# mLSTM heads 0 to 2: a head's squares are added on GpSimd before the f32 sums

## The chip, the cores and the metric

The kernel runs on one core of one Trainium2 chip. Its metric is the device time of one execution in microseconds; the kernel before takes 1200.73 us (median of three runs, 1200.3 to 1201.46). The core has TensorE (matmuls, called PE in the profile, with PEld for the loading of weights), VectorE (DVE), ScalarE (ACT), GpSimd (POOL) and SyncE (SP, which issues loads).

## The reference

The program is a two-layer encoder on 512 tokens of width 1024. Layer A mixes tokens by an mLSTM with four heads of width 192 beside a cross-attention on 256 memory tokens; layer B by band attention beside the same kind of cross-attention; each layer ends in a gated MLP with a causal convolution. The change touches the mLSTM alone. For each head and token it computes a numerator of 192 values and a denominator, divides, and normalises the 192 values by their root mean square:

```
num = einsum(s, v) + inter * einsum(q, c)          # 192 values a token
den = sum(s) + inter * einsum(q, n)
h   = num / maximum(abs(den), exp(-m))
hm  = h * rsqrt(mean(h * h) + EPS)                 # mean over the 192 values
out = hm * head_gain * sigmoid(o)
```

Division and normalisation together need two sums for each token: the sum of the squares of the 192 numerators, and the square of the denominator. The kernel computes one factor from both, as rsqrt(sum/192 + EPS * max(den^2, floor)), and multiplies the gated numerators with it.

## The kernel before

Activations lie with features in the partitions (128) and tokens in the columns (512). Matrices are f32, split into a high and a low part (`split`, L133: ScalarE casts the high part at L134, VectorE subtracts the low part at L135), and a product is three matmuls (`mm3`, L171, lines 173 to 175).

A head is the generator `mlstm_head(h)` (L1136). Its 192 values are one full tile of 128 rows and half a tile of 64, which it shares with its neighbour head. `weighted_scores` makes the weighted scores of a block of 128 key tokens (broadcast of the row terms at L1147, Exp at L1149, causal cut on GpSimd at L1151, score products, split). `products` (L1166) multiplies them with the values into two PSUM banks `nums`. Bank 0 holds 128 numerators. Bank 1 holds 64 numerators and, in its other 64 rows, 64 copies of the denominator, since the value tile has 64 columns of ones there. Which half is which depends on the head being odd; `rs` is the half with numerators.

Then come the steps that the change is about. ScalarE squares both banks (L1187), VectorE multiplies them with the output gate (L1189). TensorE sums the squares over the partitions, for four token tiles T: at L1194 and L1195 two f32 matmuls of 128x128 squares with a two-column constant `mcf` add up in `st`. Column 0 receives the sum of the 192 squares, column 1 the mean of the 64 squared copies of the denominator. `mcf[:, 0]` is 1 in column 0 for all rows; `mcf[:, 1]` and `mcf[:, 2]` have 1 in column 0 for the half with numerators and 1/64 in column 1 for the other. In the profile an f32 matmul is two instructions (two passes). From `st` VectorE computes the factor on 128x4 elements (L1199 to L1201, `rsqrt` at L217 with lines 220 to 226), and two diagonal matrices (L235). TensorE broadcasts them (`spread`, L244, matmuls at L248), and VectorE multiplies the gated numerators with the result (L1208) and splits it.

TensorE's gaps are filled with projections. `weave(job, filler, each)` (L204) advances the filler by `each` steps for every yield of the job, or by `each` times the number that is yielded. A step of a projection (`project`, L177) is three matmuls of 512 columns. The filler of heads 0 to 2 is one chain of 112 steps: query and key tiles with a convolution (`qk_tile`, L1095, taps at L1103, Silu at L1104), output gates (`o_tile`), and the queries of the memory attention (`head_queries`, L495, memsets on GpSimd at L498). Head 0 takes 1.4 steps a yield, head 1 1.125, the memory attention between heads 1 and 2 1.463, head 2 1.417; what is left runs behind head 2. Head 3 is filled with parts of the output projection. In this part of the program a scheduler orders the instructions of each engine by its estimates; the written order gives the priority. The MLPs later are ordered by hand.

Buffers are rings: 8 of the kind "t" (128x512 in SBUF: squares, Exp, convolution, diagonals), three PSUM banks "mm" for projections, three "sc", two "tr" (the `nums`).

Of the kernel before, what the change touches and what calls it, by code (L numbers as in the profile page):

```python
# [12 lines left out]
AF = mybir.ActivationFunctionType  # L13
ALU = mybir.AluOpType
AX = mybir.AxisListType

P = 128
D = 1024
S = 512
# [4 lines left out]
AH = 4  # L24
# [31 lines left out]
def trunk(  # L56
# [18 lines left out]
    nc = tc.nc  # L75
    V, A, G = nc.vector, nc.scalar, nc.gpsimd
# [10 lines left out]
    def sb(tag, shape, dtype=F32):  # L87
        count[0] += 1
        return pool.tile(shape, dtype, tag=tag, name=f"{tag}{count[0]}", bufs=bufs[tag])

    def ps(tag):
        count[0] += 1
        return psum.tile([P, S], F32, tag=tag, name=f"p{tag}{count[0]}", bufs=pbufs[tag])

    def small(n=4):
        return sb("s", [P, 32])[:, :n]
# [12 lines left out]
        out=maskf, in_=maskf, pattern=[[1, P]], base=0, channel_multiplier=-1,  # L109
# [10 lines left out]
    mcf = cpool.tile([P, 3, 2], F32, name="mcf")  # L120
# [8 lines left out]
    HEADS = (slice(0, HD), slice(HD, P))  # L129
# [3 lines left out]
    def split(hi, lo, src, on_act=True, pinned=False):  # L133
        high = A.copy(hi, src) if on_act else V.tensor_copy(hi, src)  # L134
        low = V.tensor_tensor(out=lo, in0=src, in1=f(hi), op=ALU.subtract)  # L135
        if pinned:
            pin(high)
            pin(low)
# [32 lines left out]
    def mm3(o, lh, ll, rh, rl, first, last, more=False):  # L171

        nc.tensor.matmul(o, lh, rh, start=first, stop=False, skip_group_check=more)  # L173
        nc.tensor.matmul(o, lh, rl, start=False, stop=False, skip_group_check=more)  # L174
        nc.tensor.matmul(o, ll, rh, start=False, stop=last, skip_group_check=more)  # L175
# [41 lines left out]
    def rsqrt(y, v):  # L217
        n = v.shape[-1]
        yi = y.bitcast(I32)
        V.tensor_scalar(yi, v.bitcast(I32), 1, None, op0=ALU.logical_shift_right)  # L220
        V.tensor_scalar(yi, yi, -1, 0x5F3759DF, op0=ALU.mult, op1=ALU.add)
        t = small(n)
        for _ in range(3):
            V.tensor_mul(t, y, y)
            V.scalar_tensor_tensor(t, t, -0.5, v, op0=ALU.mult, op1=ALU.mult)
            V.scalar_tensor_tensor(y, t, 1.5, y, op0=ALU.add, op1=ALU.mult)

    def diagonal(c):

        cs = [sb("s", [P, 32], F32R)[:, :TT] for _ in range(2)]  # L230
        split(*cs, c, on_act=False)
        dgs = []
        for c in cs:
            dg = sb("t", [P, S], F32R)
            V.tensor_tensor(  # L235
                out=dg.rearrange("p (a b) -> p a b", a=TT),
                in0=ident.unsqueeze(1).to_broadcast([P, TT, P]),
                in1=f(c).unsqueeze(2).to_broadcast([P, TT, P]),
                op=ALU.mult,
            )  # L240
            dgs.append(dg)
        return dgs

    def spread(dgs, tag):  # L244

        o = ps(tag)
        for i, dg in enumerate(dgs):
            nc.tensor.matmul(o, onesr, dg, start=i == 0, stop=i == 1)  # L248
        return o
# [262 lines left out]
    def head_scores(o, h, q, tsl, k, c, first, keys_first=False):  # L512

        for i, part in enumerate(q):
            a, b = part[h][:, tsl], k[h][:, c]
            if keys_first:
                a, b = b, a
            nc.tensor.matmul(o, a, b, start=first and i == 0, stop=i == 1)  # L518
# [491 lines left out]
    e, u, c, r = (cpool.tile([P, TT, AH], F32, name=f"gate{i}") for i in range(4))  # L1010
# [125 lines left out]
    def mlstm_head(h):  # L1136
        hp, odd = divmod(h, 2)
        sh = 3 * hp + 1
        full = 3 * hp + 2 * odd
        rs = slice(HD, P) if odd else slice(0, HD)  # L1140
        pt = sb("pt", [P, 5 * S], F32R)

        def weighted_scores(s):
            n = S - s * P
            sl = slice(s * P, (s + 1) * P)
            r = ps("sc")
            nc.tensor.matmul(r[:, :n], sels[s % 2][:, h, :], rp[s // 2][:, s * P :], start=True, stop=True)  # L1147
            e = sb("t", [P, S])
            A.activation(e[:, :n], r[:, :n], AF.Exp, bias=acol[:, s, h : h + 1])  # L1149

            G.affine_select(  # L1151
                out=e[:, :P], in_=e[:, :P], pattern=[[1, P]], base=0, channel_multiplier=-1,
                compare_op=ALU.is_ge, fill=0.0,
            )
            yield
            o = ps("sc")
            kf, qf = ks[full], qs[full]
            mm3(o[:, :n], kf[0][:, sl], kf[1][:, sl], qf[0][:, s * P :], qf[1][:, s * P :], True, False)
            head_scores(o[:, :n], odd, qs[sh], slice(s * P, S), ks[sh], sl, False, True)
            V.scalar_tensor_tensor(e[:, :n], o[:, :n], DH**-0.5, e[:, :n], op0=ALU.mult, op1=ALU.mult)  # L1160
            split(pt[:, RO[s] : RO[s + 1]], pt[:, 1280 + RO[s] : 1280 + RO[s + 1]], e[:, :n])
            yield

        nums = []

        def products(s):  # L1166
            if not nums:
                nums.extend(ps("tr") for _ in range(2))
            for o, c in zip(nums, (3 * P, 2 * P) if odd else (0, P)):
                mm3(  # L1170
                    o[:, s * P :], vh[hp][s][:, c : c + P], vl[hp][s][:, c : c + P],
                    pt[:, RO[s] : RO[s + 1]], pt[:, 1280 + RO[s] : 1280 + RO[s + 1]], s == 0, s == TT - 1,
                )
            yield

        yield from weighted_scores(0)
        yield from weighted_scores(1)
        yield from weighted_scores(2)
        yield from products(0)
        yield from weighted_scores(3)  # L1180
        yield from products(1)
        yield from products(2)
        yield from products(3)
        sqs = []
        for o, j, r in ((nums[0], full, slice(0, P)), (nums[1], sh, rs)):
            sq = sb("t", [P, S])
            A.activation(sq, o, AF.Square)  # L1187
            sqs.append(sq)
            V.tensor_tensor(out=og[j][r, :], in0=o[r, :], in1=og[j][r, :], op=ALU.mult)  # L1189
        yield  # L1190
        st = ps("sc")
        for T in range(TT):
            sl = slice(T * P, (T + 1) * P)
            nc.tensor.matmul(st[:, 2 * T : 2 * T + 2], sqs[0][:, sl], mcf[:, 0, :], start=True, stop=False)  # L1194
            nc.tensor.matmul(st[:, 2 * T : 2 * T + 2], sqs[1][:, sl], mcf[:, 1 + odd, :], start=False, stop=True)  # L1195
            yield 0.581
        st = st[:, : 2 * TT].rearrange("p (t c) -> p t c", c=2)
        z, fc = small(), small()
        V.tensor_tensor(out=z, in0=st[:, :, 1], in1=floor2[:, :, h], op=ALU.max)  # L1199
        V.tensor_scalar(z, z, EPS, 1e-35, op0=ALU.mult, op1=ALU.max)  # L1200
        V.scalar_tensor_tensor(z, st[:, :, 0], 1.0 / DH, z, op0=ALU.mult, op1=ALU.add)  # L1201
        rsqrt(fc, z)
        dg = diagonal(fc)
        yield 2.673
        fb = spread(dg, "sc")
        yield
        for j, r in ((full, slice(0, P)), (sh, rs)):
            V.tensor_tensor(out=og[j][r, :], in0=fb[r, :], in1=og[j][r, :], op=ALU.mult)  # L1208
            if mixes[j] is None:
                mixes[j] = sb("u", [P, S], F32R), sb("u", [P, S], F32R)  # L1210
            split(mixes[j][0][r, :], mixes[j][1][r, :], og[j][r, :])
# [8 lines left out]
    fill = chain(a_tiles(2), a_memory_queries(0), a_tiles(3, 4), a_tiles(5), a_memory_queries(1))  # L1220
    memkv = load_memory_kv(0)
    weave(mlstm_head(0), fill, 1.4)
    until(lambda: og[2] is not None, fill)
    weave(mlstm_head(1), fill, 1.125)
    until(lambda: memq[0] is not None, fill)
    weave(memory_attention(memq[0], memkv, 0, mixes), fill, 1.463, 4)
    until(lambda: og[4] is not None, fill)
    weave(mlstm_head(2), fill, 1.417)
    run(fill)
    reload_x()  # L1230
# [30 lines left out]
    for j in range(KT):  # L1261
        wh, wl = weights(rows(ffn_w_down[0], j * P, P, FT - LAST, FT), LAST, P)
        o = ps("mm")
# [252 lines left out]
```

## Time and profile before

| | us |
|---|---|
| median of three runs | 1200.73 |
| the profiled execution | 1202.01 |
| its span | 1200.3 |
| head 0, first row broadcast (L1147) to the second gated product (L1208) | 104.9 to 137.4 |
| sums of heads 0, 1, 2 and 3, first start | 125.0, 150.0, 206.3, 244.1 |

The profile shows one execution. A row of a timeline gives the start in us from the span's start, the duration in us, engine, line, operation, output<-input, shapes, and how many instructions are merged; in brackets the idle time ahead of it and what ended it. A row of waits gives who waited for whom, the total in us, how often, and the longest. A row of groups ends with the total busy time, the mean in ns, and the idle time ahead of the group.

### The profile page before, as it was taken

Reading aid. Unit: us, or ns where it says so; the run is one execution under the profiler, and the core shown is the slowest. Engines: PE = TensorE matmul, PEld = TensorE weight load, DVE = VectorE, ACT = ScalarE, POOL = GpSimd, SP = SyncE. Lnnn points to the kernel's source line nnn. Section 1 sums busy time; section 2 is a strip of 40 time slices with the busy share of each in tenths; the row PEclk is TensorE's granted clock in tenths of the full one; section 3 lists DMA queues with packets and bytes.
Section 4 is the critical chain, followed back from the end, with each engine's and each line's share of the span. In section 5 each row is a group of like instructions: output and inputs, shape, how many; then the busy total and the mean of one; then the engine's idle time right before and its main releaser. Section 6 shows DMA issues by size and latency. Waiting matters only on the chain.

```text
span 1200.3 us, 18274 instructions
## 1 busy us (share of the span) xinstructions
PE 1189.5 (99%) x6759; PEld 1041.8 (87%) x6759; DVE 971.2 (81%) x1810; ACT 708.8 (59%) x1276; POOL 123.5 (10%) x207
## 2 busy tenths in 40 slices
PE   9999999999999999999999999999999999999997
PEld 8988888888889989999888888888889989999986
DVE  6877687878978888888698888997897888888865
ACT  5546577654655555555565667775465555555545
POOL 1200101010021111111020000001001010111100
PEclk9999999999999999999999999999999999999999
DMA  8634222444275666665563323146326466666551
GB/s 287 210 88 123 54 54 57 146 140 132 70 175 161 155 157 161 151 144 128 146 195 111 91 70 100 54 130 202 115 88 149 106 140 141 141 138 137 121 158 70
DMA packets 199019, 155.97 MB, mean 130 GB/s; under 512 B 7864, under 2 KB 179346, under 8 KB 198930
## 3 DMA queue, kind: packets, MB, share of 16 engines
q1 hardware_dynamic: 183762, 119.73, 34.5%
q0 software_dynamic: 14592, 34.03, 13.8%
q8 instruction: 53, 0.87, 0.3%
q10 hardware_dynamic: 576, 1.05, 0.2%
q14 instruction: 36, 0.29, 0.1%
HBM read 126.27 MB, written 32.44 MB: 132 GB/s over the span
## 4 chain that ended last, share of the span: by engine, by line
PE 89%; DVE 6%; ACT 3%; DMA 2%; issue 1%; SPq 0%; ACTq 0%; DVEq 0%
PE pmm L173 14%; PE pmm L175 14%; PE pmm L174 14%; PE ptr L173 6%; PE ptr L175 6%; PE ptr L174 6%; PE pmm L783 6%; PE psc L175 4%; PE psc L173 4%; PE psc L174 4%; PE pmm L782 3%; PE psc L518 2%; DMA wr<-in_ffn_w_up_dram 1%; DVE u L135 1%; PE ptr L1343 1%; DVE wl L135 1%
## 5 line engine op out<-in xcount | busy, mean ns | idle before, releaser
L173 PE MATMUL pmm<-u,wh 128*128 128x512 f32 (+1 forms) x872 | 309.5, 355 | 0.1
L175 PE MATMUL pmm<-u,wl 128*128 128x512 f32 (+1 forms) x872 | 306.4, 352 | 0.0
L174 PE MATMUL pmm<-u,wh 128*128 128x512 f32 (+1 forms) x872 | 306.2, 351 | 0.1
L135 DVE TENSOR_TENSOR wl<-wr,wh 128x1024 fp32r<-128x1024 f32 (+3 forms) x172 | 199.4, 1161 | 55.8 <-ACT wh L134 53.9
L134 ACT CAST wh<-wr 128x1024 fp32r<-128x1024 f32 (+3 forms) x172 | 171.6, 1002 | 107.9 <-PE pmm L174 45.8
L175 PEld LDWEIGHTS pmm<-u,wl 128*128 128x128 f32 x872 | 164.5, 189 | 21.1
L174 PEld LDWEIGHTS pmm<-u,wh 128*128 128x128 f32 x872 | 164.7, 189 | 18.2 <-DVE u L135 0.8
L173 PEld LDWEIGHTS pmm<-u,wh 128*128 128x128 f32 x872 | 164.6, 189 | 18.0 <-ACT u L134 0.5
L173 PE MATMUL ptr<-u,wh 128*128 128x512 f32 x272 | 106.7, 392 | 0.0
L175 PE MATMUL ptr<-u,wl 128*128 128x512 f32 x272 | 106.1, 390 | 0.0
L174 PE MATMUL ptr<-u,wh 128*128 128x512 f32 x272 | 105.9, 389 | 0.0
L751 POOL DMA_DIRECT2D xspill<-t x64 | 55.5, 867 | 461.3 <-ACT t L750 450.3
L134 ACT CAST u<-pt 128x512 fp32r<-128x512 f32 x102 | 62.8, 616 | 45.9 <-DVE pt L873 45.8
L135 DVE TENSOR_TENSOR u<-pt,u 128x512 fp32r<-128x512 f32 x102 | 70.1, 688 | 11.2 <-ACT u L134 8.5
L175 PE MATMUL psc<-u,wl 128*128 128x256 f32 (+1 forms) x232 | 76.1, 328 | 0.2
L173 PE MATMUL psc<-u,wh 128*128 128x256 f32 (+1 forms) x232 | 76.2, 328 | 0.0
L174 PE MATMUL psc<-u,wh 128*128 128x256 f32 (+1 forms) x232 | 75.9, 327 | 0.0
L783 PE MATMUL pmm<-u,u 128*128 128x512 f32 x192 | 69.6, 397 | 0.0
L935 ACT ACTIVATE t<-t 128x512 f32<-128x512 f32 x34 | 21.5, 632 | 79.4 <-DVE t L658 79.4
L819 DVE TENSOR_TENSOR t<-t,pmm 128x256 f32<-128x256 f32 x72 | 30.1, 418 | 45.2 <-ACT t L817 45.1
L658 DVE SCALAR_TENSOR_TENSOR t<-t,cols,t 128x511 f32<-128x511 f32 x80 | 59.4, 743 | 3.7 <-ACT t L665 3.7
L750 ACT COPY t<-ptr 128x512 f32<-128x512 f32 x64 | 37.4, 585 | 42.1 <-PE ptr L175 42.1
(298 smaller groups left out, 2673.1 us busy)
## 6 DMA issues: line engine op xcount, KB each, us to landing
wr<-in_ffn_w_up_dram SPq DMA_DIRECT2D x54, 512.0 KB, 4.4
wr<-in_ffn_w_down_dram SPq DMA_DIRECT2D x38, 512.0 KB, 4.1
pt<-in_ffn_w_up_dram SPq DMA_DIRECT2D x34, 512.0 KB, 6.5
xspill<-t POOLq DMA_DIRECT2D x64, 256.0 KB, 5.3
wr<-in_a_w_in_dram SPq DMA_DIRECT2D x20, 512.0 KB, 3.9
xspill<-u POOLq DMA_DIRECT2D x32, 256.0 KB, 2.7
u<-xspill SPq DMA_DIRECT2D x32, 256.0 KB, 5.5
wr<-in_w_kv_dram SPq DMA_DIRECT2D x12, 512.0 KB, 3.9
```

The source lines that it names most:

```text
L134: high = A.copy(hi, src) if on_act else V.tensor_copy(hi, src)
L135: low = V.tensor_tensor(out=lo, in0=src, in1=f(hi), op=ALU.subtract)
L173: nc.tensor.matmul(o, lh, rh, start=first, stop=False, skip_group_check=more)
L174: nc.tensor.matmul(o, lh, rl, start=False, stop=False, skip_group_check=more)
L175: nc.tensor.matmul(o, ll, rh, start=False, stop=last, skip_group_check=more)
L518: nc.tensor.matmul(o, a, b, start=first and i == 0, stop=i == 1)
L658: V.scalar_tensor_tensor(acc[:, n:], src[:, : S - n], self.fw[:, c * FT + j : c * FT + j + 1], acc[:, n:], op0=ALU.mult, op1=ALU.add,)
L750: A.copy(t, o)
L751: G.dma_start(xspill[j], t, accum_op=ALU.add)
L782: nc.tensor.matmul(r[:, :H], w[1][:, k], p[i - 1][:, :H], start=False, stop=False, skip_group_check=True)
L783: nc.tensor.matmul(r, w[0][:, k], p[i - 1], start=False, stop=k == n - 1, skip_group_check=True)
L819: V.tensor_tensor(out=o, in0=o, in1=r[:, H:], op=ALU.add)
```

## The change

The two banks' squares are no longer summed by two matmuls a token tile. The squares of bank 1 stay in a 128-row tile `sq`. For heads 0 to 2, the squares of bank 0 are written in two halves of 64 rows into the rows of `sq` that hold numerators (tile `part`, rows `rs`), and GpSimd adds each half to them. Each of those 64 rows of `sq` then holds the sum of three squares, and one matmul a token tile is left. Head 3 keeps two tiles of squares and two matmuls.

Three things move with it. The gating products of VectorE stand behind all squares, bank 1 ahead of bank 0 in the built order. The yield ahead of the sums is 4 instead of 1 for heads 0 to 2. The sums of the four token tiles stand in one row, and the yield of 0.581 behind each of them is one of 2.324 behind the last.

```diff
-        sqs = []
+        sq = sb("t", [P, S])
+        A.activation(sq, nums[1], AF.Square)
+        terms = [(sq, mcf[:, 1 + odd, :])]
+        if h < AH - 1:
+
+            for half in HEADS:
+                part = sb("t", [P, S])
+                A.activation(part[rs, :], nums[0][half, :], AF.Square)
+                G.tensor_tensor(out=sq[rs, :], in0=sq[rs, :], in1=part[rs, :], op=ALU.add)
+        else:
+            part = sb("t", [P, S])
+            A.activation(part, nums[0], AF.Square)
+            terms.append((part, mcf[:, 0, :]))
         for o, j, r in ((nums[0], full, slice(0, P)), (nums[1], sh, rs)):
-            sq = sb("t", [P, S])
-            A.activation(sq, o, AF.Square)
-            sqs.append(sq)
             V.tensor_tensor(out=og[j][r, :], in0=o[r, :], in1=og[j][r, :], op=ALU.mult)
-        yield
+        yield 4 if h < AH - 1 else 1
         st = ps("sc")
         for T in range(TT):
             sl = slice(T * P, (T + 1) * P)
-            nc.tensor.matmul(st[:, 2 * T : 2 * T + 2], sqs[0][:, sl], mcf[:, 0, :], start=True, stop=False)
-            nc.tensor.matmul(st[:, 2 * T : 2 * T + 2], sqs[1][:, sl], mcf[:, 1 + odd, :], start=False, stop=True)
-            yield 0.581
+            for i, (t, c) in enumerate(terms):
+                nc.tensor.matmul(st[:, 2 * T : 2 * T + 2], t[:, sl], c, start=i == 0, stop=i == len(terms) - 1)
+        yield 2.324
```

## Prediction

> **What bounds the kernel now.** I read the page's busy shares and chain first, then the busy times of the stretch that holds the four heads, then what TensorE waited for in it.
>
> ```profile
> span 1200.3 us, 18274 instructions
> PE 1189.5 (99%) x6759; PEld 1041.8 (87%) x6759; DVE 971.2 (81%) x1810; ACT 708.8 (59%) x1276; POOL 123.5 (10%) x207
> PE 89%; DVE 6%; ACT 3%; DMA 2%; issue 1%; SPq 0%; ACTq 0%; DVEq 0%
> 84.00:256.00 172.00, 171.61 (x873) 144.27 (x872) 134.29 (x273) 110.69 (x191) 10.72 (x22) 1.00 0.31 87
> PE psc L173 <- ACT t L1149: 0.2, 1, 0.2
> PEld psc L173 <- ACT t L1149: 0.9, 2, 0.6
> PEld psc L248 <- DVE t L235: 0.6, 2, 0.3
> ```
>
> TensorE is busy 99% of the span and carries 89% of the chain. In the 172 us of the heads it is idle for 0.39 us at a granted clock of 1.00; its one wait is 0.2 us, the weight loads' longest are 0.6 and 0.3 us. So a matmul taken out here shortens the program by what it holds TensorE, and a wait put in lengthens it by as much: there is no idle time left to swallow one.
>
> **The matmuls that go.** This is TensorE around head 0's sums: the head's last numerator matmul, then projection matmuls (pmm), then the sums (L1194, L1195), two passes to an f32 matmul. Columns: start, duration.
>
> ```profile
> 122.76 0.28 PE L175 MATMUL ptr<-pt,u 128*128 128x128 f32 x1
> 122.88 0.44 PE L173 MATMUL pmm<-u,wh 128*128 128x512 f32 x1
> ...
> 124.78 0.40 PE L175 MATMUL pmm<-u,wl 128*128 128x512 f32 x1
> 125.01 0.28 PE L1194 MATMUL psc<-mcf,t 128*128 128x2 f32 x2
> ...
> 125.38 0.47 PE L173 MATMUL pmm<-u,wh 128*128 128x512 f32 x1
> 125.69 0.39 PE L174 MATMUL pmm<-u,wh 128*128 128x512 f32 x1
> ...
> 126.15 0.28 PE L1194 MATMUL psc<-mcf,t 128*128 128x2 f32 x2
> ...
> 126.96 0.47 PE L173 MATMUL pmm<-u,wh 128*128 128x512 f32 x1
> 127.28 0.39 PE L174 MATMUL pmm<-u,wh 128*128 128x512 f32 x1
> ...
> 127.74 0.28 PE L1194 MATMUL psc<-mcf,t 128*128 128x2 f32 x2
> 127.88 0.36 PE L1195 MATMUL psc<-mcf,t 128*128 128x2 f32 x2
> 128.10 0.47 PE L173 MATMUL pmm<-u,wh 128*128 128x512 f32 x1
> 128.42 0.39 PE L174 MATMUL pmm<-u,wh 128*128 128x512 f32 x1
> ```
>
> Between two projection matmuls lies 0.23 us (124.78 to 125.01). A group of four passes holds the next matmul up by 125.38 - 125.01 = 0.37, and the one behind it by 0.31 - 0.23 = 0.08: 0.45 us. The group of eight costs 126.96 - 126.15 = 0.81 and 0.32 - 0.23 = 0.09: 0.90. The third costs 0.36 + 0.09 = 0.45. Sum per head 1.80 us for 16 passes. Afterwards a head of 0 to 2 has eight passes in one row: 0.90. That takes off 3 x 0.90 = 2.70 us. Head 3 keeps 16 passes, but in one row instead of two, with one change-over (0.09) less. **Together -2.79 us**, all of it on the path.
>
> **The new way to the sums.** In the built order 21 projection matmuls now lie between a head's last numerator matmul and its sums, where 9, 6 and 9 lay before. Counted from the start of that last matmul (122.76), the sums' turn comes at 0.12 + (124.78 - 122.88) + 13 x 0.23 = 5.0 us, their weight load 0.23 before: 4.77. By then three ScalarE squares and two GpSimd adds must be done, in order. For prices on ScalarE, VectorE and GpSimd:
>
> ```profile
> 122.74 1.09 ACT L1187 ACTIVATE t<-ptr 128x512 f32<-128x512 f32 x2 [1.89 <-PE ptr L175]
> 155.00 1.28 ACT L1104 ACT_TABLE_LOAD   x1 [3.26 <-DVE s L1201]
> 156.29 0.63 ACT L1104 ACTIVATE t<-t 128x512 f32<-128x512 f32 x1
> 158.28 0.62 ACT L134 CAST u<-t 128x512 fp32r<-128x512 f32 x1
> L498 POOL MEMSET u<- 64x512 f32 x24 | 12.8, 533 | 46.9 <-PE pmm L175 23.5 <-PE psc L518 13.5 <-PE ptr L1365 7.9
> L108 POOL TENSOR_SCALAR_AFFINE_SELECT maskf<-maskf 128x128 f32<-128x128 f32 x1 | 0.3, 284 | 0.0
> L106 POOL MEMSET maskf<- 128x128 f32 x1 | 0.2, 204 | 0.0
> L1505 POOL MEMSET const-float32-1.0<- 128x1 f32 x1 | 0.1, 108 | 0.0
> 140.06 1.25 POOL L1151 TENSOR_SCALAR_AFFINE_SELECT t<-t 128x128 f32<-128x128 f32 x1 [0.57 <-ACT t L1149]
> 140.01 1.15 DVE L135 TENSOR_TENSOR pt<-t,pt 128x512 fp32r<-128x512 f32 x2
> ```
>
> No GpSimd add stands in the trace. From below, it is not cheaper than the memset of the same shape, which reads nothing: 0.53 us. From GpSimd's rows on 128 elements: the memset costs (204 - 108)/128 = 0.75 ns an element for writing, the select (284 - 108)/128 = 1.38 for reading one input and writing, so a read is 0.63. Two reads and a write give 2.01 ns x 512 + 108 = **1.14 us**, the value I take; two whole one-input passes, 2 x (1.38 x 512 + 108) = 1.63 us, are the upper end. [...]
>
> The other unknown is whether VectorE holds GpSimd up. The quoted select took 1.25 us instead of the 0.28 of L108; it ended at 141.31, just after two VectorE operations with both inputs in SBUF (140.01 to 141.16). So an add can lose what such an operation takes. [...]
>
> Heads 0 and 2. The square of the second bank can start at 0.28 + 0.02 = 0.30 and takes 0.60; with the spacing of L1187 (two in 1.09, so 0.49) the two halves end at 1.40 and 1.90. Adds: 1.45 to 2.59 and 2.64 to 3.78. One in each of these heads could last 1.63 us and still meet 4.77. VectorE's operations there read PSUM (the gating products, the convolution taps), the next split of weights comes behind them. **Cost 0**, covered by 0.95 us of matmuls; without that cover it would cost 2 x any excess over 1.63 us per head.
>
> Head 1. In the built order a table load and a Silu stand between the first and second square, and a cast between second and third. First square 0.30 to 0.90, table load 0.80 to 2.08, Silu 2.09 to 2.72, second square to 3.20, cast to 3.77, third square to 4.30 (each overlapping its forerunner by 0.1 as L1187 does). Adds: 3.25 to 4.39, and 4.44 to 5.58; the sums' weight load at 5.63 instead of 4.77: **0.9 us of wait**. VectorE's low half of that cast, both inputs in SBUF, is ready at 3.8, while the first add runs, and comes between the adds for another 0.6. I take 1.4 us, the ends being 0 (a table load that is through early) and 0.9 + 2 x 0.49 + 0.6 = 2.5.
>
> **Behind the sums.** The VectorE chain from the sums to the diagonals that the broadcast (L248) multiplies, head 1:
>
> ```profile
> 153.32 0.16 DVE L1199 TENSOR_TENSOR s<-psc,floor 128x4 f32<-128x4 f32 x1 [0.22 <-PE psc L1195]
> 153.40 0.74 DVE L1103 SCALAR_TENSOR_TENSOR t<-pmm,cols,t 128x510 f32<-128x510 f32 x1
> 154.06 0.16 DVE L1200 TENSOR_SCALAR s<-s 128x4 f32<-128x4 f32 x1
> 154.17 0.75 DVE L1103 SCALAR_TENSOR_TENSOR t<-pmm,cols,t 128x509 f32<-128x509 f32 x1
> 154.83 0.15 DVE L1201 SCALAR_TENSOR_TENSOR s<-psc,s 128x4 f32<-128x4 f32 x1
> 155.02 0.17 DVE L220 TENSOR_SCALAR s<-s 128x4 int32<-128x4 int32 x1
> 157.48 1.29 DVE L235 TENSOR_TENSOR t<-ident,s 128x512 fp32r<-128x512 f32 x2
> 158.69 1.22 DVE L135 TENSOR_TENSOR wl<-wr,wh 128x1024 fp32r<-128x1024 f32 x1
> 159.82 0.69 DVE L135 TENSOR_TENSOR u<-t,u 128x512 fp32r<-128x512 f32 x1
> ```
>
> Before, from L1199 to the end of the first diagonal: 157.48 + 0.68 - 153.32 = 4.84 us. Afterwards head 1 has inside this chain three taps (0.66 each with the step to the next), two splits of weights (1.13) and one of a cast (0.61): 0.08 + 2 x 1.13 + 3 x 0.66 + 2 x 0.11 + (157.48 - 155.02) + 0.61 + 0.68 = 8.29. TensorE has 36 projection matmuls to put there, 8.28 us. A wait of some **0.2 us** for L248. Head 0 keeps 29 of 30, head 2 its 24, with the same members in the chain; where the split of weights now stands earlier in head 2's, it waits for its high half: **0.2 us**. Ends for all three: 0 and 1.
>
> **What costs nothing.** Three more 64-row squares on ScalarE: 1.5 us, in a stretch where it works 110.69 of 172. The 12 filler steps that the longer yields bring forward: they are matmuls that come anyway, and head 2's order still has matmuls on both sides of its sums; were they used up, each missing step would bare 3 x 0.23 us of waiting. SP's loads keep their order. On GpSimd a head's adds stand ahead of the next head's selects and the memsets of queries; these are due only after L248, microseconds later. [...] The extra buffer of "t" adds no wait on the squares in the built order.
>
> **Sum.** -2.79 + 1.4 + 0.2 + 0.2 = -1.0 us. The profiled execution took 1202.01 us (span 1200.3); it would take 1201.0. The median of the three runs is 1200.73, 1.28 below that execution; I put the difference on it: **1199.7 us**.
>
> **Rivals.** First, no new wait: everything meets its turn in head 1 too, for instance because the table is loaded while TensorE still multiplies. Then -2.79 stays: 1197.9. Heads 0 and 2 with 0.95 us to spare speak for it; head 1's table load, which the order puts between its squares, against it.
>
> Second, slower: the add itself. If it takes g, head 1 waits 1.5 + 2 (g - 1.14), heads 0 and 2 each 2 (g - 1.63). With the 0.4 behind the sums the gain is used up at g = 1.6; at g = 2.0 the kernel is 0.2% slower; at 2.2 it is -2.79 + 0.4 + 3.6 + 2.3 = +3.5: 1204.2. For it: the select at 140.06 that took over four times its time; against it: the three GpSimd rows, which give 1.14.
>
> Third, the removed passes held nobody: then only the waits remain, +1.8, 1202.5. Against it: each group moves the next matmul by 0.36 to 0.81 us.
>
> **How the numbers follow.** About 0.2% (2.4 us) is what a measurement can tell from no change. The forecast, net -2.3 to +1, has 0.49; no wait 0.27; a slow add 0.16; removed passes free 0.05; 0.03 for waits elsewhere in the reordered stretch, above. Faster: the first rival, 0.27. Slower: the slow add and half of the rest, 0.18. Same: 0.55. The likeliest case's own range is 1198.4 to 1201.8. The range for 8 in 10 reaches from the full saving with no wait, 1197.8, to head 1's upper end (2.5) with 1 us at L248 and some of the slow add: 1202.6.
>
> **What would show it.** Sums: 20 f32 matmuls, not 32, in 40 passes; 8 passes of 0.81 us in heads 0 to 2. Six GpSimd adds of about 1.14 us. One wait of TensorE's weight load on GpSimd, near 150 us, of 0.9 to 1.5 us; none in heads 0 and 2. A small wait of L248 on L235 behind head 1. The stretch from 256 us on unchanged but earlier by 1 us. Wrong: adds over 1.63 us, waits on GpSimd in all three heads, or none at all.

## The result, and the profile after

The changed kernel takes 1202.38 us (median of 21 runs, 1201.33 to 1203.95); the kernel before, run beside it, 1200.74 (21 runs, 1200.16 to 1202.85). The ratio is 1.0012, with a 95% interval of 1.0007 to 1.0018: slower by 1.6 us. The forecast was 1199.7, so 1 us faster. The time lies inside the range and within the 0.2% that was called "same", but on the other side of zero, and above the 1198.4 to 1201.8 of the likeliest case. The profiled execution shown here took 1203.74 us, so it is one of the slower of the 21.

The page's opening lines of the changed kernel, its chain by engines, and the busy times of the stretch that was shown of before (time, then PE, PEld, DVE, ACT, POOL, then the granted clock, the DMA share and GB/s):

```profile
span 1202.0 us, 18245 instructions
PE 1190.2 (99%) x6735; PEld 1042.8 (87%) x6735; DVE 973.0 (81%) x1810; ACT 708.4 (59%) x1277; POOL 130.5 (11%) x213
PE 93%; DVE 3%; ACT 2%; issue 1%; DMA 0%; POOL 0%; SPq 0%; DVEq 0%; ACTq 0%
```

```profile
84.00:256.00 172.00, 169.77 (x837) 141.83 (x836) 132.85 (x269) 108.14 (x190) 17.74 (x28) 0.98 0.30 86
```

TensorE has 24 instructions fewer (6735 instead of 6759) and still bounds the kernel. But in the same 172 us it is now busy for 169.77 instead of 171.61, and the mean granted clock is 0.98, not 1.00. The waits of that stretch, TensorE's own first, then those of its weight loads (total, times, longest):

```profile
PE psc L1204 <- POOL t L1192: 1.6, 1, 1.6
PE ptr L174 <- DVE pt L135: 0.3, 1, 0.3
PE psc L248 <- DVE t L235: 0.2, 1, 0.2
PE pmm L174 <- DVE u L135: 0.2, 1, 0.2
...
PEld psc L1204 <- POOL t L1192: 2.0, 1, 2.0
PEld psc L248 <- DVE t L235: 0.9, 2, 0.6
```

One wait of the sums (L1204) on GpSimd, as forecast, in head 1 only. TensorE's timeline around it shows the rest of the story:

```profile
154.61 0.39 PE L175 MATMUL pmm<-u,wl 128*128 128x512 f32 x1
156.63 1.55 PE L1204 MATMUL psc<-mcf,t 128*128 128x2 f32 x8 [1.63 <-POOL t L1192]
158.04 0.78 PE L173 MATMUL pmm<-u,wh 128*128 128x512 f32 x1
158.62 0.63 PE L174 MATMUL pmm<-u,wh 128*128 128x512 f32 x1
...
163.31 0.63 PE L173 MATMUL pmm<-u,wh 128*128 128x512 f32 x1
163.74 0.45 PE L174 MATMUL pmm<-u,wh 128*128 128x512 f32 x1
164.02 0.39 PE L175 MATMUL pmm<-u,wl 128*128 128x512 f32 x1
```

The wait is 156.63 - 154.61 - 0.23 = 1.79 us. Behind it the projection matmuls start every 0.43 us instead of 0.23, until 163.7. The reason stands in the busy times by microsecond (granted clock third from the right):

```profile
155.00:156.00 1.00, 0.00 (x1) 0.00 (x0) 0.97 (x2) 0.97 (x2) 1.00 (x1) 1.00 0.00 0
156.00:157.00 1.00, 0.37 (x4) 0.37 (x4) 0.17 (x1) 0.60 (x1) 1.00 (x2) 1.00 0.00 0
157.00:158.00 1.00, 1.00 (x7) 1.00 (x7) 0.00 (x0) 0.00 (x0) 0.56 (x2) 0.50 0.00 0
...
163.00:164.00 1.00, 1.00 (x4) 0.78 (x3) 0.93 (x5) 0.13 (x1) 0.00 (x0) 0.58 0.03 8
164.00:165.00 1.00, 1.00 (x6) 0.82 (x5) 0.24 (x3) 0.00 (x0) 0.00 (x0) 1.00 0.00 0
...
1198.00:1199.00 1.00, 0.00 (x0) 0.00 (x0) 0.05 (x1) 0.02 (x1) 0.00 (x0) 0.53 0.07 29
```

The clock is halved from 157.00 to 163.84 (0.58 over the last microsecond is 0.84 of it at half). That is 6.84 us at half speed, 3.42 us lost: more than the wait itself. (The last row, after the last matmul, is used further down.)

The sums of the other heads, and head 3's:

```profile
127.09 0.95 PE L1204 MATMUL psc<-mcf,t 128*128 128x2 f32 x8
127.90 0.49 PE L173 MATMUL pmm<-u,wh 128*128 128x512 f32 x1
...
212.04 0.95 PE L1204 MATMUL psc<-mcf,t 128*128 128x2 f32 x8
212.85 0.49 PE L173 MATMUL pmm<-u,wh 128*128 128x512 f32 x1
...
246.65 1.84 PE L1204 MATMUL psc<-mcf,t 128*128 128x2 f32 x16
248.35 0.49 PE L173 MATMUL ptr<-u,wh 128*128 128x512 f32 x1
```

Eight passes take 0.81 us and wait for nothing in heads 0 and 2. Head 3's sixteen in one row take 1.70; before, two rows of 0.81.

GpSimd: the group of all six adds, and then the timelines of the engines that meet in head 1:

```profile
L1192 POOL TENSOR_TENSOR t<-t,t 64x512 f32<-64x512 f32 x6 | 8.0, 1340 | 24.6 <-ACT t L1191 15.4 <-issue 9.0
```

```profile
153.60 2.97 POOL L1192 TENSOR_TENSOR t<-t,t 64x512 f32<-64x512 f32 x2 [9.01 <-issue]
...
150.92 1.28 ACT L1104 ACT_TABLE_LOAD   x1
152.22 0.63 ACT L1104 ACTIVATE t<-t 128x512 f32<-128x512 f32 x1
152.87 0.59 ACT L1191 ACTIVATE t<-ptr 64x512 f32<-64x512 f32 x1
...
154.13 0.59 ACT L1191 ACTIVATE t<-ptr 64x512 f32<-64x512 f32 x1
...
154.14 1.30 DVE L135 TENSOR_TENSOR u<-t,u 128x512 fp32r<-128x512 f32 x1 [2.57 <-ACT u L134]
```

An add takes 1.28 to 1.29 us; in head 1 the second took 1.60 (six in 8.0 us). The table load and the Silu stand ahead of the second square, as the order said, and VectorE's low half of the cast ran beside the adds.

### The profile page after: what moved, and what is told of

Read it like the earlier page. It is cut to its first block, busy times and chain, and to the rows that moved or that the text cites. A ratio compares the mean times of both kernels' runs of the same rounds, so it can differ in the third digit from the quotient of the medians.

```text
span 1202.0 us, 18245 instructions
## 1 busy us (share of the span) xinstructions
PE 1190.2 (99%) x6735; PEld 1042.8 (87%) x6735; DVE 973.0 (81%) x1810; ACT 708.4 (59%) x1277; POOL 130.5 (11%) x213
## 3 DMA queue, kind: packets, MB, share of 16 engines
q10 hardware_dynamic: 576, 1.05, 0.2%
## 4 chain that ended last, share of the span: by engine, by line
PE 93%; DVE 3%; ACT 2%; issue 1%; DMA 0%; POOL 0%; SPq 0%; DVEq 0%; ACTq 0%
PE pmm L173 15%; PE pmm L174 15%; PE pmm L175 15%; PE ptr L174 6%; PE ptr L175 6%; PE ptr L173 6%; PE pmm L783 6%; PE psc L175 5%; PE psc L173 5%; PE psc L174 5%; PE pmm L782 3%; PE psc L518 2%; PE ptr L1352 1%; PE ptr L1373 1%; PE ptr L1374 1%
```

## The experiments

The stretch used below runs from head 0's first row broadcast (L1147) to the first broadcast L248 behind head 3's, which holds all four heads: 104.95 to 287.93 before, 182.98 us, and 104.30 to 290.54 after, 186.24. Its start lies between 103.66 and 105.92 us in the profiles of this document; the stretch itself doesn't contain that difference. All times are set against runs of the kernel before on the same chip.

First question: is it head 1's wait, and the clock behind it? Four edits of the changed kernel. In all of them the rest of the change stays: the gating products behind the squares, and each head's sums in one row.

**Head 1 as before, heads 0 and 2 changed.**

```diff
-        if h < AH - 1:
+        if h in (0, 2):
...
-        yield 4 if h < AH - 1 else 1
+        yield 4 if h in (0, 2) else 1
```

> The changed kernel, but head 1 keeps its two sums per token tile and its yield of 1; heads 0 and 2 keep the GpSimd adds. Theory A (head 1's wait of 1.8 us and the half clock behind it, 3.2 us, are the whole loss): no wait at the sums, granted clock 1.00 from 136 to 170 us, and two heads' saving of 0.90 each: about 1198.9 us. Rival B (the adds, or the reordering they bring, cost in every head): two thirds of the loss stay, about 1201.8 us.

1201.58 us against 1200.97, ratio 1.0000 (0.9992 to 1.0009). The wait is gone and the clock is 1.00 throughout. The stretch is 0.42 us shorter than before, where two heads' removed matmuls alone make 1.80. So the wait and the clock are not all of the loss: some 1.4 us went into the new order.

**Only head 1 changed.**

```diff
-        if h < AH - 1:
+        if h == 1:
...
-        yield 4 if h < AH - 1 else 1
+        yield 4 if h == 1 else 1
```

> Only head 1 has the GpSimd adds, heads 0 and 2 are as before. The order puts 18 matmuls instead of 21 between its numerators and its sums. Theory A: the wait is 2.5 us, the clock halves behind it for 3.2 us, less one saving of 0.90: 1200.7 + 2.5 + 3.2 - 0.9 = 1205.5 us. Rival B (a third of the loss in each head): 1201.3 us.

1201.36, ratio 1.0004 (0.9995 to 1.0013). The high figure was a miss for a reason of its own: in this order no table load stands between head 1's squares, so there is no long wait to test (0.4 us on the weight load). The stretch is 0.57 us longer than before, though a head's 0.90 was taken off: again about 1.5 us in the order.

**A longer yield ahead of head 1's sums:** 27 projection matmuls there instead of 21, and in a second kernel (a yield of 6) 24.

```diff
-        yield 4 if h < AH - 1 else 1
+        yield (4, 7, 4, 1)[h]
```

> The changed kernel with a yield of 7 instead of 4 ahead of head 1's sums: 27 projection matmuls instead of 21 lie before them (1.4 us more), and 31 instead of 36 behind them. Theory A: the wait at the sums shrinks from 1.8 to 0.4 us, the clock stays at 1.00, and of the 2.8 us saved about 1.9 remain, some 0.5 going to a later broadcast in head 1: 1198.9 us. Rival B (adds and reordering): no change against the changed kernel, 1202.4. Rival C (any wait at the sums halves the clock): about 1201.

> As with the yield of 7, but 6: 24 projection matmuls before head 1's sums, so a wait of about 1.1 us there. If the clock falls only behind waits near 1.8 us, 1199.5 us with a clock of 1.00; if 1.1 us is enough, about 3 us more, 1202.5, with a stretch at 0.50. Rival B: 1202.4 without such a stretch.

With 27, 1199.73 us (1199.32 to 1200.2), ratio 0.9991 (0.9982 to 1.0000). Little of the wait is left, and the clock is 1.00:

```profile
156.15 0.39 PE L175 MATMUL pmm<-u,wl 128*128 128x512 f32 x1
156.83 1.05 PE L1204 MATMUL psc<-mcf,t 128*128 128x2 f32 x8 [0.29 <-POOL t L1192]
```

Six matmuls, 1.4 us of work that comes anyway, turned 1.6 us above before into 1.2 below. With 24 the profile shows a wait of 157.04 - 155.69 - 0.23 = 1.12 us and a clock of 1.00:

```profile
155.69 0.39 PE L175 MATMUL pmm<-u,wl 128*128 128x512 f32 x1
157.04 1.05 PE L1204 MATMUL psc<-mcf,t 128*128 128x2 f32 x8 [0.96 <-POOL t L1192]
```

The median was 1200.62, but the runs spread from 1199.76 to 1203.69: six up to 1200.62, the others up to 3 us above. The mean granted clock is on record for every run; here it is 0.997 in the three slowest and 0.998 or 0.999 in the other eight. So a wait of 1 us costs more than its length in some executions only.

Second question: what is the order worth by itself, what the adds, and is the lower clock a chance of one profile? Four kernels.

**The changed kernel again.**

> The changed kernel once more, unchanged. Theory A (the wait at head 1's sums starts a drop of the granted clock, as in the profile after, and the two together cost 1.8 + 3.2 us): median 1202.4 again, and a profile with a wait of 1.6 to 1.9 us of L1204 on GpSimd near 155 us and, behind it, 3 to 7 us at a granted clock near 0.5. Theory B (that drop was a chance of one profiled execution, the loss lies elsewhere): the profile shows the wait and no drop, the median is 1202.4 all the same.

1202.50 (1201.5 to 1204.09), ratio 1.0013 (1.0004 to 1.0023). The profile has the same wait (156.97 - 154.96 - 0.23 = 1.78 us) and again the lower clock, for half as long, and later:

```profile
158.00:159.00 1.00, 1.00 (x6) 0.84 (x6) 0.94 (x2) 0.00 (x0) 0.00 (x0) 0.98 0.00 0
159.00:160.00 1.00, 1.00 (x4) 0.80 (x3) 1.00 (x3) 0.00 (x0) 0.00 (x0) 0.50 0.00 0
...
162.00:163.00 1.00, 1.00 (x5) 0.78 (x5) 0.83 (x6) 0.94 (x2) 0.00 (x0) 0.81 0.34 99
...
1196.00:1197.00 1.00, 0.00 (x0) 0.00 (x0) 0.75 (x1) 0.72 (x1) 0.00 (x0) 0.81 0.00 0
```

That is 158.96 to 162.38: 3.42 us at half, 1.71 lost. The stretch is 184.56 us, 1.58 longer than before; in the first profile it was 3.26, and the difference is one such piece.

**Two sums a tile as before, in the new order, without adds.**

```diff
-        if h < AH - 1:
+        if False:
```

> All heads keep two tiles of squares and two sums a token tile, and no GpSimd adds; what stays of the change is the order: longer yield ahead of the sums, the sums in one row. No matmul is removed, and TensorE has nothing to wait for. Theory A (the wait and the clock behind it are the loss): before's time less seven change-overs of 0.09, so 1200.3. Theory C (the new order by itself costs 1 to 2 us, which head 1 alone and head 1 left out both seemed to show): 1201.5 to 1202.5.

1202.92 (1202.25 to 1203.13), ratio 1.0017 (1.0008 to 1.0026). Nothing is removed, TensorE waits for no sum, the clock is 1.00, and it is 2.1 us slower. Theory C stands: the order costs. In the profile the cost is spread over many small delays, the longest of which are 0.50 us at head 3's product and this one in the memory attention (180.41 to 181.03, 0.39 too late):

```profile
180.41 0.39 PE L173 MATMUL pmm<-u,wh 128*128 128x512 f32 x1
181.03 0.70 PE L587 MATMUL ptr<-ident,t 128*128 128x128 f32 x4 [0.24 <-DVE t L578]
```

**The changed kernel without its adds.**

```diff
                 A.activation(part[rs, :], nums[0][half, :], AF.Square)
-                G.tensor_tensor(out=sq[rs, :], in0=sq[rs, :], in1=part[rs, :], op=ALU.add)
```

> The GpSimd adds are left out (the factor then lacks the squares of bank 0), all else stays: 16 passes less for heads 0 to 2 together with one row of sums, and the squares on ScalarE. Theory A: -2.79 and a wait of at most 0.4 us at head 1's sums, which come after the table load but no longer after two adds; no drop of the clock: 1198.2 to 1198.6. Theory C (the order costs 1 to 2 us): 1199.3 to 1200.3.

1199.22, ratio 0.9986 (0.9977 to 0.9995): 1.6 us faster, where 2.70 were taken off. Its stretch is 1.41 us shorter than before, so the order takes 1.29. TensorE's own waits there:

```profile
PE ptr L174 <- DVE pt L135: 0.3, 1, 0.3
PE psc L248 <- DVE t L235: 0.2, 1, 0.2
```

L248 starts 0.29 us late in head 1 and 0.36 in head 2, a product of head 3 0.49, all three waiting for VectorE; the rest is in pieces of 0.2 and less.

**One more add ahead of head 1's two.**

```diff
-                A.activation(part[rs, :], nums[0][half, :], AF.Square)
+                A.activation(part[rs, :], nums[0][half, :], AF.Square, scale=0.5**0.5 if h == 1 and half is HEADS[0] else 1.0)
+                if h == 1 and half is HEADS[0]:
+                    G.tensor_tensor(out=part[rs, :], in0=part[rs, :], in1=part[rs, :], op=ALU.add)
```

> One more GpSimd add of the same shape ahead of head 1's two (the half's square is scaled by 1/2 on ScalarE and doubled by an add, which leaves the sum as it is); TensorE's order is that of the changed kernel. The wait of L1204 should grow from 1.8 to 3.1 us. Theory A: the drop of the clock is there in the profile again, and as it lasts a fixed stretch the time is 1202.4 + 1.3 = 1203.7; should the drop grow with the wait, 1205. Theory B (nothing hangs on the wait but its own length): 1203.7 too, but no drop of the clock in the profile.

1204.26 (1202.36 to 1205.06), ratio 1.0027 (1.0017 to 1.0037). The profiled execution, 1202.41, is one of the two lowest, and it shows the wait without any drop of the clock:

```profile
154.63 0.39 PE L175 MATMUL pmm<-u,wl 128*128 128x512 f32 x1
157.74 1.05 PE L1206 MATMUL psc<-mcf,t 128*128 128x2 f32 x8 [2.71 <-POOL t L1194]
```

```profile
159.00:160.00 1.00, 1.00 (x6) 0.84 (x5) 1.00 (x1) 0.00 (x0) 0.00 (x0) 1.00 0.00 0
```

So a wait of 2.9 us need not lower the clock. The other six runs are 1.2 to 2.7 us longer than this one, and their granted clocks are lower: 0.995 to 0.997 in five of them and 0.998 in one, against 0.999 in the two lowest. One 1.71 piece is 0.0014 of the mean clock, so five of the six had one piece or two.

Third question: does a wait of that kind lower the clock where nothing else is changed? The kernel before, with GpSimd adds put ahead of head 1's sums. With one (and, in the other two kernels, a scale of 1/2 or 0.125**0.5 and a loop of two or three adds):

```diff
-            A.activation(sq, o, AF.Square)
+            A.activation(sq, o, AF.Square, scale=0.5**0.5 if h == 1 and j == sh else 1.0)
+            if h == 1 and j == sh:
+                G.tensor_tensor(out=sq, in0=sq, in1=sq, op=ALU.add)
```

> The kernel before with one GpSimd add put ahead of head 1's sums (the second square is scaled by 1/2 on ScalarE and doubled by the add, so the sum is as it was); TensorE's order is that of before, matmul for matmul, and no matmul is removed. By rows: the two squares end 1.4 to 1.9 us after the last numerator matmul, the add 1.3 later, the sums' turn comes at 1.5: a wait of 1.3 to 1.8 us. Theory A (a wait of this length also halves the granted clock for 0, 3.4 or 6.6 us, by where it falls): before + 1.5 + 0 to 3.2, median 1203.5 to 1204, runs spread over more than 2 us, and in most profiles some us near 0.5 behind the wait. Theory B (only the wait's own length): 1202.1 to 1202.7, clock 1.00.

> The kernel before with two GpSimd adds in a row ahead of head 1's sums (the second square is scaled by 1/4 and doubled twice), no matmul removed; TensorE's order differs by one step of a projection beside these sums. One add gave a wait of 0.57 us and +0.6; a second adds 1.29: a wait of 1.9 us. Theory A (a wait of this length lets the granted clock halve behind it in most executions, for 3.4 or 6.6 us): 1200.8 + 1.9 + 1.4 = 1204.1, the runs spread over more than 2 us, the lowest near 1202.5. Theory B (a wait costs its own length): 1202.7, runs within 1.5 us.

> As before, with three adds: a wait of 3.0 to 3.2 us. Theory A: 1200.8 + 3.1 + 1.8 = 1205.7, the lowest near 1203.8, spread over more than 2 us. Theory B: 1203.9, runs within 1.5 us.

One add: 1201.41 against 1200.80, ratio 1.0006 (0.9997 to 1.0014), clock 1.00; the wait was only 0.57 us (the sums on the first square alone still come before it), so it didn't yet test theory A. Two adds: 1204.29 against 1201.70, ratio 1.0019 (1.0010 to 1.0028). Three: 1206.78, ratio 1.0042 (1.0028 to 1.0056, from five runs). Two adds, TensorE's timeline and the busy times:

```profile
149.92 0.40 PE L174 MATMUL pmm<-u,wh 128*128 128x512 f32 x1
151.29 0.38 PE L1198 MATMUL psc<-mcf,t 128*128 128x2 f32 x2 [0.98 <-POOL t L1190]
```

```profile
153.00:154.00 1.00, 1.00 (x7) 0.91 (x5) 0.10 (x1) 0.00 (x0) 0.00 (x0) 0.72 0.31 52
...
156.00:157.00 1.00, 1.00 (x4) 0.80 (x3) 0.83 (x5) 1.00 (x1) 0.00 (x0) 0.57 0.00 0
```

and three:

```profile
151.95 0.40 PE L173 MATMUL pmm<-u,wh 128*128 128x512 f32 x1
154.84 0.38 PE L1198 MATMUL psc<-mcf,t 128*128 128x2 f32 x2 [2.49 <-POOL t L1190]
```

```profile
157.00:158.00 1.00, 1.00 (x5) 0.75 (x5) 0.93 (x4) 0.00 (x0) 0.00 (x0) 0.65 0.05 12
...
160.00:161.00 1.00, 1.00 (x4) 0.77 (x4) 0.83 (x6) 0.66 (x2) 0.00 (x0) 0.64 0.00 0
```

Waits of 1.14 and 2.66 us, shorter than expected, and behind each a piece at half clock: 153.44 to 156.86 and 157.30 to 160.72, 3.42 us both. The balance of the stretch, in us against the 182.98 of before (the wait beyond the 0.23 spacing; half of the time at half clock; the rest is what remains):

| kernel | stretch | removed | wait | clock | rest |
|---|---|---|---|---|---|
| before, one add | +0.62 | 0 | 0.57 | 0 | 0.05 |
| before, two adds | +2.92 | 0 | 1.14 | 1.71 | 0.07 |
| before, three adds | +4.49 | 0 | 2.66 | 1.71 | 0.12 |
| changed, first profile | +3.26 | -2.70 | 1.79 | 3.42 | 0.75 |
| changed, again | +1.58 | -2.70 | 1.78 | 1.71 | 0.79 |
| changed, a third add | +1.72 | -2.70 | 2.88 | 0 | 1.54 |
| changed, 24 matmuls ahead | -0.31 | -2.70 | 1.12 | 0 | 1.27 |
| changed, 27 matmuls ahead | -1.05 | -2.70 | 0.45 | 0 | 1.20 |
| changed, no adds | -1.41 | -2.70 | 0 | 0 | 1.29 |

In the kernel before, wait and clock account for all but 0.1 us: theory A holds there, with nothing removed and next to nothing reordered. In the changed order a rest of 1.2 to 1.5 us stays, and 0.5 less where the clock was halved: at half clock TensorE comes later to L248 (168.79 to 169.01 in the first profile, no delay), so VectorE is in time for it. That is 0.29 of the 0.5; the other 0.2 is not traced.

**Does another order or engine save the gain?** Yields of 3, 7, 3; the sums of four tiles apart again (a yield of 0.581 behind each, with 27 matmuls ahead in head 1); head 1's adds on VectorE, and the same with a yield of 6:

```diff
-        yield 4 if h < AH - 1 else 1
+        yield (3, 7, 3, 1)[h]
...
-        yield 2.324
+            yield 0.581
...
-                G.tensor_tensor(out=sq[rs, :], in0=sq[rs, :], in1=part[rs, :], op=ALU.add)
+                (V if h == 1 else G).tensor_tensor(out=sq[rs, :], in0=sq[rs, :], in1=part[rs, :], op=ALU.add)
```

> The changed kernel with yields of 3, 7, 3 ahead of the sums of heads 0 to 2 instead of 4, 4, 4. In this order no table load stands between head 1's squares, and 15, 27 and 18 projection matmuls stand ahead of the sums. Theory A: no wait in heads 1 and 2, 0 to 0.4 in head 0, clock 1.00; -2.70 and some 0.6 to 1.2 of small waits elsewhere: 1199 to 1199.6. Theory C (the reordering costs about 2 us whatever the yields): 1200.1 to 1200.8.

> As the variant with 27 matmuls ahead of head 1's sums (1199.73), but the sums of the four token tiles stand apart again, with a yield of 0.581 behind each, as before. If the row of sums with everything else behind it is what makes TensorE wait for the diagonals (L248) and for splits, this gives less of that: 1199.3, at the price of up to nine more change-overs of 0.09 (0.8): 1199.3 to 1200.1. If the place of the sums does not matter beyond the change-overs: 1200.5.

> Head 1's two adds on VectorE, the rest as in the changed kernel. By the rows of splits an add takes 0.7 there, not 1.3: the second ends near 5.2 to 5.7 us after the last numerator matmul, the sums' turn with 22 projection matmuls ahead comes at 5.0: a wait of 0.2 to 0.7 us. Theory A: no drop of the clock behind so short a wait, so the changed kernel less 1.2 of wait and less 1.6 of clock: 1199.5 to 1200.1, runs within 1.2 us. Theory B (the clock has no part): 1202.4 - 1.2 = 1201.2.

> Head 1's adds on VectorE and 24 projection matmuls ahead of its sums (22 with the wait of 0.4 us). No wait is left there, clock 1.00. Of the changed kernel's other small waits (L248, head 3's product) nothing is touched. Theory A: 1199.64 - 0.5 = 1199.1, runs within 1.2 us. Theory C (a shift of order gives back as much as the wait was): 1199.6 or more.

Yields of 3, 7, 3: 1200.64 against 1200.80 (ratio 0.9989 to 1.0007). No long wait, clock 1.00, and still only 0.05 us off the stretch, as theory C had it and theory A had not: L248 waits three times, 0.8 us together, the memory attention 0.5, the sums 0.4. Sums apart: 1199.84 (0.9984 to 1.0001), no different from one row. VectorE in head 1: 1199.64 (1198.68 to 1200.48), ratio 0.9988 (0.9979 to 0.9997); an add takes 0.69 us there, and the wait is short:

```profile
PE psc L1204 <- DVE t L1192: 0.4, 1, 0.4
```

With the longer yield as well: 1200.39 against 1201.70, ratio 0.9990 (0.9982 to 0.9999): the last 0.4 us of wait was not turned into time, against theory A's 1199.1. Head 1's adds on VectorE, or 27 matmuls ahead of its sums, both measure some 1.2 us below before (the interval of the second just reaches no difference) and 2.8 below the change as made.

## Why the prediction was wrong, point by point

- **The removed matmuls.** Right for heads 0 to 2: eight passes of 0.81 us, nothing in between. Head 3's change-over of 0.09 was not saved: 1.70 us in one row against twice 0.81. So -2.70, not -2.79.
- **Heads 0 and 2 at no cost.** Right: no wait at their sums. Head 0's two adds took 2.66 us from 123.58 on, beside a gating product of VectorE with one input in PSUM (124.15) that took 0.69, the median of those products before.
- **The add.** Mis-sized: 1.14 us taken from three rows of GpSimd, 1.28 measured. The meeting with VectorE, priced at 0.6 us from the row of one select, was there: 1.60 us for that add, and 1.30 instead of 0.69 for VectorE's subtraction.
- **Head 1's wait.** Right in place and cause, 1.79 us instead of 1.4, inside the ends of 0 to 2.5.
- **Behind the sums.** 0.2 + 0.2 us at L248 were forecast; the first profile shows no delay behind head 1 and 0.2 us of idle time behind head 2 (0.37 beyond the 0.23 spacing), but the first only since the clock was low ahead of it. What was missing is that the moved work delays TensorE in many other places as well: 1.2 to 1.5 us in this order, 2.3 in the two-sums kernel. The step that said the moved filler "are matmuls that come anyway", and cost nothing, is wrong: the matmuls come anyway, but what feeds them has less time. The waits for VectorE that were named above show this for 1.14 of the 1.29 us; for the small delays it is argued.
- **The step that failed** is the first: "a wait put in lengthens it by as much". A wait of 1 us or more costs its length and, in four of the six profiles with such a wait, 1.71 or 3.42 us more, because the granted clock halves behind it (what stood ahead of each halving is counted in the last section). No term of the sum and no rival had that.

In numbers, from -1.0 to +1.6: 1.71 for one piece at half clock, 0.39 for the longer wait, 0.35 to 0.39 for the order (0.75 to 0.79 instead of 0.4), 0.09 for head 3: 2.6. The three possible counts also give the spread of the changed kernel's runs: without a piece 1200.8 - 2.70 + 1.79 + 1.3 = 1201.2, and with a rest of 0.8 in place of 1.3 it is 1202.4 with one and 1204.1 with two; measured are 1201.33 at the lowest, 1202.38 and 1202.50 as medians, 1204.09 at the highest. The two profiles had one and two. For the runs without a profile the granted clocks bear it out in the main: beside the experiments, none of the 116 runs of the kernel before is under 0.998, while ten of the 21 runs of the changed kernel are at 0.997 or below, and the four at 0.995 or 0.996 all took 1203.64 us or more. They don't explain every run: one of 1203.21 us has 0.999.

Of the rivals, none came true. The slow add needed 1.6 us an add to use up the gain, and 1.28 was measured; the third (removed passes that held nobody) gave nearly the right time, 1202.5, by luck and for the wrong reason: without adds, and so without the wait, the removed passes did shorten the stretch, by 1.41 us.

## What to carry to other kernels

Where TensorE is busy without a gap, price a new wait with the clock that it may cost: keep it short, by more matmuls ahead or by a faster engine (waits of 0.45 and 0.57 us lowered nothing here, nor did 1.12 and 2.88, but 1.14, 1.78, 1.79 and 2.66 did), or expect that many executions lose 1.71 or 3.42 us on top. With two-column passes beside it, even 0.98 us of idle time had half clock behind it (before, two adds). A small saving on the bound engine has to be larger than what the reordering itself costs, which a kernel with the new order and without the saving shows directly (here 1.3 to 2.3 us against 2.7). And look at the granted clock by microsecond behind every new wait: the page's row of the clock in 40 slices showed one digit changed in one profile of the changed kernel, and none in the other.

## What the runs showed of the hardware that was not expected

The pieces at half clock are 3.42 us long or twice that. In the changed kernel's first profile the piece starts at 157.00, and the clock falls again after the last matmul at 1198.06 (0.53 in the row shown): 1041.06 us apart. In windows of 0.1 us that piece reaches from 157.006 to 163.832, so half of it is 3.413 us, and 1041.06 is 305 times that. In the second profile the distance is 1196.62 - 158.96 = 1037.66, 304 times 3.413; with two and three adds 1044.48, 306 times. The idle time alone does not tell whether a piece follows: behind two adds 0.98 us had one behind it, 1.63 us in the first profile two, and 2.71 us in the profile with the third add none.

What does go with the pieces in these profiles is how many columns the matmuls work through in the 3.413 us ahead of them. For the table each profile is divided into windows of 3.413 us, counted back from the clock's fall after the last matmul, and the matmuls are counted in matmuls of 512 columns, each spread over the 0.23 us to the next one (0.43 at half clock). In the profile of before and the first of the changed kernel the median window holds 14.5. The first five rows are all the windows with half clock behind them but those at the end of the matmuls; the last three are windows near them that were followed by full clock:

| kernel | window | matmuls | clock in it | clock behind it |
|---|---|---|---|---|
| before, three adds | 153.89 to 157.31 | 3.5 | full | half |
| changed, again | 155.55 to 158.96 | 4.4 | full | half |
| before, two adds | 150.02 to 153.44 | 4.6 | full | half |
| changed, first profile | 153.59 to 157.00 | 5.5 | full | half |
| changed, first profile | 157.00 to 160.41 | 5.2 | half | half |
| before, two adds | 153.44 to 156.85 | 6.0 | half | full |
| changed, a third add | 153.50 to 156.91 | 6.0 | full | full |
| changed, a third add | 156.91 to 160.32 | 7.0 | full | full |

In the profile of before and the first of the changed kernel, 685 of the 689 windows from 20 us on hold 7.1 or more and are followed by full clock; the other four are this first profile's two in the table and the two at the end of the matmuls (0 and 1.4), all followed by half clock. At the start it was otherwise: a window of before holds 3.7 (2.74 to 6.15) and one of the changed kernel 4.5 (3.41 to 6.83), and both are followed by full clock. A pass of the sums works through two columns only, so the sums count for next to nothing here: behind two adds ten such passes stood in the window of 4.6, with the 0.98 us of idle time, while the 2.71 us with the third add were split over the windows of 6.0 and 7.0. The count was made on these traces after the runs, and no run was built to test it: it tells what went with the pieces here, not what makes them.
